# Banded attention heads of a hybrid transformer layer, put into one written order, with the division behind the values

## The chip, the cores and the metric

The kernel runs on one core of a Trainium2 chip. The metric is the device time of one launch in microseconds (us), the median of the runs. Engines are named as in the profile: PE (TensorE matmul), PEld (its weight load), DVE (VectorE), ACT (ScalarE), POOL (GpSimd) and SP (SyncE, which here only issues transfers).

## The reference, cut to what matters

One layer over 512 latent tokens with 256 context tokens: a modulated norm and one input projection, differential attention (group A, 4 heads), banded attention (group B, 8 heads of 64 columns, 2 key heads), one output projection, a second norm, a router that takes 4 of 32 experts, the experts, a last norm. The change lies in group B:

```python
def window_gqa_latent(q, k, v, k_ctx, v_ctx, sink):      # blocks of 128 queries
    ...
    s_loc = jnp.einsum('bnqkgd,bnjkd->bnkgqj', qbk, kband)       # own block and its neighbours
    s_ctx = jnp.einsum('bnqkgd,bjkd->bnkgqj', qbk, k_ctx)        # 256 context tokens
    ...
    s_loc = jnp.where(valid[None, :, None, None], s_loc, MASK_VALUE)
    ...
    p = jax.nn.softmax(jnp.concatenate([s_loc, s_ctx, sink_col], axis=-1), axis=-1)
    p_loc = p[..., :3 * W].astype(v.dtype)
    p_ctx = p[..., 3 * W:-1].astype(v.dtype)
    o = (jnp.einsum('bnkgqj,bnjkd->bnqkgd', p_loc, vband)
         + jnp.einsum('bnkgqj,bjkd->bnqkgd', p_ctx, v_ctx))
    return o.reshape(B, S, WA_OUT)
```

`x = x + g1 * (concatenate([ya, yb]) @ w_out)` follows, and the router and the experts work on its norm.

## The kernel before

Group B is done in 16 units (n, m): n is the block of 128 queries (0 to 3), m the pair of heads (0 to 3). A unit has 512 keys (`nk`) at n = 0 and 3, and 640 at n = 1 and 2, in 4 or 5 blocks of 128 (256 context tokens and the band). Every 32-bit operand stands as a high part and a low part, so a product is made of several matmuls.

- `scores_B(n, m)`: for each of the two heads a score product of queries `qB` with the keys `kB`. The first matmul of a pair has 128 rows (high query and low query parts against the high keys), the second has 64 rows and takes the low keys, `kB[rw, 2]`. Masks (`mprev`, `mnext`) are added by matmuls with `identb`. The sink goes into column `nk` of the scores by a one-column copy, on DVE for one head and on ACT for the other. DVE takes the negated maximum (`nmB`), ACT the exponential with its sum (`pB`, `rsB`), DVE the reciprocal of the sum. Then `pB` is multiplied by it, one head on ACT and the other on DVE.
- `turn_B`: PE transposes `pB` in groups of two key blocks (8 transposes of 128x128 into one `tp` tile), ACT writes the high part `pTh`, DVE the low part `pTl`. There are two `tp` tiles.
- `mix_B`: PE multiplies the values `vB` with both parts into `o`.
- `put_B` after every second unit: ACT copies (`yB`), DVE adds, and both split the result into `two`, the left operand of the output projection.
- `out_proj(n, kb)` multiplies `two` by row block kb of `w_out`: 6 matmuls of 512 columns. The row blocks are loaded by SP into `wo` (two buffers), split by ACT (`CAST`) and DVE in `prep_out` into `wp` or `w`.
- Beside the units the loop carries the group-A output (`start_Y`), the second norm (`norm2`), the router (`route_T`, `route` with `choose`, `rank`) and the gates' bias (`turn_gates`, `start_acc`) of earlier query blocks.

The order on PE, DVE and ACT is set by a planner wherever `pinned[0]` is empty, and by the order of the code where it names engines (P, V, S). Before, it is empty in the loop over the units, and the planner also brings the scores of units (0,1) and (0,2), six of the eight `wo` splits and the first three `out_proj` into the last part of group A. After the loop come the rest of the router, the gathering of tokens, and the experts.

Of the kernel before, what the change touches and what calls it, by code (L numbers as in the profile page):

```python
# [10 lines left out]
F32 = mybir.dt.float32  # L11
F32R = mybir.dt.float32r
# [10 lines left out]
T = 512  # L23
# [14 lines left out]
def tile_block(ctx: ExitStack, tc: tile.TileContext, a: dict, out: bass.AP, dbg=None):  # L38
# [64 lines left out]
    def ps_pj():  # L103
        return ps.tile([128, 512], F32, name="pj", bufs=2)
# [704 lines left out]
    def scores_B(n, m):  # L809

        b0, b1 = max(n - 1, 0), min(n + 2, 4)
        L = (b1 - b0) * 128
        nk = C + L
        g = m // 2
        rw = slice(g * 64, g * 64 + 64)
        q = qT[n]
        own = n + m < KN["own"]
        if own:
            assert nk == 512
            sv = [ps_pj() for _ in range(2)]  # L820
        else:
            s = sc_tile(KN["sB"])
            sv = [s[:, 0:TA], s[:, TA:2 * TA]]
        for i in range(2):
            hd, s = 2 * m + i, sv[i]
            cuts = [(0, C), (C, nk)] if i == 1 or nk == 512 else [(0, C), (C, 512), (512, nk)]
            masks = []
            if n > 0:
                masks.append((mprev, C))
            if n < 3:  # L830
                masks.append((mnext, nk - 128))
            ksl = lambda x0, x1: slice(T + x0, T + x1) if x0 < C else slice(b0 * 128 + x0 - C, b0 * 128 + x1 - C)
# [6 lines left out]
            if not own and KN["snk"] == "P":  # L839
                PE.matmul(s[:, nk:nk + 1], ones3, sink3[:, hd:hd + 1], start=True, stop=True)  # L840
        nm = bp.tile([128, 2], F32, name="nmB", bufs=4)
        rs = bp.tile([128, 2], F32, name="rsB", bufs=4)
        w = nk if own else nk + 1
        for i in range(0 if own or KN["snk"] == "P" else 2):
            (V.tensor_copy if KN["snk"][i] == "V" else S.copy)(sv[i][:, nk:w], sinkB[:, 2 * m + i:2 * m + i + 1])
        for i in range(2):
            V.tensor_reduce(nm[:, i:i + 1], sv[i][:, 0:w], axis=AX.X, op=OP.max, negate=True)
        if own:
            es = bp.tile([128, 3, 2], F32, name="esB", bufs=1)
            V.tensor_scalar_mul(es[:, 0], sinkB[:, 2 * m:2 * m + 2], -1.0)  # L850
            V.tensor_tensor(nm, nm, es[:, 0], op=OP.min)
            V.tensor_add(es[:, 1], nm, sinkB[:, 2 * m:2 * m + 2])
            S.activation(es[:, 2], es[:, 1], AF.Exp)
        pp = []
        for i in range(2):
            p = bp.tile([128, 641], F32, name="pB", bufs=5)
            S.activation(p[:, 0:w], sv[i][:, 0:w], AF.Exp, bias=nm[:, i:i + 1], accum_out=rs[:, i:i + 1])
            pp.append(p)
        if own:
            V.tensor_add(rs, rs, es[:, 2])  # L860
        V.reciprocal(rs, rs)
        for i in range(2):
            if KN["scB"][i] == "S":
                S.activation(pp[i][:, 0:nk], pp[i][:, 0:nk], AF.Copy, scale=rs[:, i:i + 1])
            else:
                (V if KN["scB"][i] == "V" else G).tensor_scalar(pp[i][:, 0:nk], pp[i][:, 0:nk], rs[:, i:i + 1], 1.0,
                                                             op0=OP.mult, op1=OP.mult)
        return pp, [4, 5] + list(range(b0, b1))

    def turn_B(pp, bl):  # L870

        w = len(bl) * 256
        tp = ps_tp().rearrange("p a b -> p (a b)")
        for i, x in enumerate(bl):
            for j in range(2):
                PE.transpose(tp[:, (2 * i + j) * 128:(2 * i + j + 1) * 128], pp[j][:, x * 128:(x + 1) * 128], ident)
        pt = pair(bp, [128, 512], "pT", 2)
        split(pt[0][:, 0:w], pt[1][:, 0:w], tp[:, 0:w])
        return pt
# [8 lines left out]
    def put_B(g, o, y):  # L888
# [40 lines left out]
    cur = scores_B(0, 0)  # L929
# [72 lines left out]
    Gt = lp.tile([128, E], F32, name="Gt")  # L1002
# [10 lines left out]
    fill = lp.tile([128, E * 3], F32, name="fill")  # L1013
    V.memset(fill, 0.0)
# [42 lines left out]
    def norm2(t):  # L1057
        t1 = lp.tile([128, D], F32, name="t1", bufs=2)
        for f in range(2):
            add_out(t, f, t1)  # L1060
        late = V if t == 3 else G
        gp2(t1, x1[t], G2B, OP.mult)
        sq = lp.tile([128, 4, 128], F32, name="ya", bufs=1).bitcast(BF16).rearrange("p a b -> p (a b)")
        ss = lp.tile([128, 1], F32, name="ss2", bufs=2)
        rs = lp.tile([128, 1], F32, name="rs2", bufs=2)
        S.activation(sq, x1[t], AF.Square, accum_out=ss)
        rstd_of(rs, ss, D)

        rt[t] = t1, rs, late
# [53 lines left out]
    def enter_slots(t):  # L1123
        eq, mi, ge, gs, pr = rt.pop(t)
        pk = lp.tile([128, 4, E], F32, name="pk")
# [13 lines left out]
        V.tensor_mul(eq, eq, val[:, :, 1:2].to_broadcast([128, 4, E]))  # L1139
        V.tensor_reduce(Gt, eq.rearrange("p k e -> p e k"), axis=AX.X, op=OP.add)  # L1140
# [29 lines left out]

    for i, (n, m) in enumerate(units):
        nxt = scores_B(*units[i + 1]) if i < 15 else None
        if m % 2 == 0:
            o = ps_o()
        pp, blocks = cur
        if m == 0 and n > 0:
            start_Y(n)
        if n == 0 and m == KN["ys"][0]:
            start_Y(n, slice(0, KN["yh"]))
        if n == 0 and m == KN["ys"][1]:  # L1180
            start_Y(n, slice(KN["yh"], 4))
# [4 lines left out]
        pts = [turn_B(pp, bl) for bl in bls[:2]]
        for k, bl in enumerate(bls):
            if k == 2:
                pts.append(turn_B(pp, bl))
            if k < len(fill):  # L1190
                out_proj(fill[k][0], [fill[k][1]])
            mix_B(m, pts[k], bl, blocks, o)
        cur = nxt
        if m % 2 == 1:
            put_B(m // 2, o, Yt[n][1])
# [3 lines left out]
        if n == 0 and m == 2:  # L1199
            router_vectors()  # L1200
# [4 lines left out]
        if n > 0:  # L1205
            (norm2, route_T, route, rank)[m](n - 1)
# [651 lines left out]
```

## Time and profile before

| | us |
|---|---|
| median of 3 runs (lowest, highest) | 1682.74 (1678.67, 1683.17) |
| the profiled execution, its own time | 1678.89 |
| its span | 1677.1 |
| start of the scores of unit (0,1) | 285.87 |
| last output of group A is stored (`YA_d<-y`) | 309.61 |
| last low part of the banded heads (`two<-yB`) ends | 456.54 |
| first matmul of the experts | 485.85 |

Times in rows are microseconds from the start of the span. A row of the timeline gives start, length, engine, line, operation, tiles and shapes, and in brackets how long the engine had stood idle and what released it. Almost every row has line 52, the helper that records the operations, so one goes by the names of tiles. Matmuls are pipelined: the length of a single one holds its way through the array; what it costs in a stream is the length of a row with many of them by their count.

### The profile page before, as it was taken

How to read it: one execution, taken by the hardware profiler on the slowest of the kernel's cores; microseconds unless marked ns; L12 is line 12 of the kernel's file. 1: busy time of each engine (PE TensorE's matmuls, PEld its weight loads, DVE VectorE, ACT ScalarE, POOL GpSimd, SP SyncE). 2: the span in 40 equal slices, each digit the busy share in tenths (PEclk: the TensorE clock that was granted, in tenths of full speed). 3: DMA queues.
4: the chain of work that ended last, by engine and by line, in shares of the span. 5: the costliest groups of instructions: out<-in, count | busy, mean ns of one | idle time of the engine just before them, and what ended most of it. 6: DMA issues, size and time to landing. Idle time of an engine off the chain costs nothing. (4 is left out here: it accounts for less than half of the span.)

```text
span 1677.1 us, 20947 instructions
## 1 busy us (share of the span) xinstructions
PE 1601.9 (96%) x7464; PEld 1283.1 (77%) x7464; DVE 1482.5 (88%) x1753; ACT 1093.5 (65%) x1406; POOL 213.6 (13%) x136
## 2 busy tenths in 40 slices
PE   7899997899889999999999999999999999999995
PEld 2686775677677888888888888888888888888884
DVE  6888887556778999999999999999999999999995
ACT  6544434445556767777776777776777777677763
POOL 0000001012330111111111111111111111111011
PEclk9899997879979999999999999999999999999998
DMA  9534325611579999999999999999999999999974
GB/s 350 173 92 132 108 88 149 184 45 47 193 244 380 353 367 369 357 377 372 374 362 366 360 369 380 383 362 366 369 362 369 374 374 361 367 355 370 357 295 128
DMA packets 115698, 494.11 MB, mean 295 GB/s; under 512 B 16385, under 2 KB 39082, under 8 KB 68418
## 3 DMA queue, kind: packets, MB, share of 16 engines
q1 hardware_dynamic: 99090, 456.44, 71.2%
q0 software_dynamic: 14192, 29.00, 8.4%
q10 hardware_dynamic: 2304, 7.24, 1.2%
q8 instruction: 61, 1.00, 0.2%
q14 instruction: 51, 0.42, 0.1%
HBM read 472.91 MB, written 27.57 MB: 298 GB/s over the span
## 5 line engine op out<-in xcount | busy, mean ns | idle before, releaser
L52 PE MATMUL h<-two 128*128 128x512 f32 x1694 | 421.5, 400 | 3.0 <-ACT two L52 3.0
L52 PEld LDWEIGHTS h<-two 128*128 128x128 f32 x1694 | 315.3, 189 | 74.3 <-ACT two L52 3.9
L52 PE MATMUL h<-wp,two 128*128 128x512 f32 x1338 | 334.7, 400 | 4.1 <-DVE pk L52 4.1
L52 DVE TENSOR_TENSOR two<-wp,two 128x1024 fp32r<-128x1024 f32 x254 | 300.8, 1219 | 7.5 <-ACT two L52 7.4
L52 PEld LDWEIGHTS h<-wp,two 128*128 128x128 f32 x1338 | 249.1, 190 | 58.2 <-ACT two L52 4.3
L52 ACT CAST two<-wp 128x1024 fp32r<-128x1024 f32 x254 | 258.0, 1049 | 17.0 <-PE y L52 14.6
L52 DVE TENSOR_TENSOR wp<-wp 128x1024 fp32r<-128x1024 f32 x176 | 205.5, 1219 | 2.9 <-ACT wp L52 2.9
L52 DVE TENSOR_TENSOR two<-w,two 128x1024 fp32r<-128x1024 f32 x170 | 200.2, 1219 | 2.3 <-ACT two L52 2.3
L52 POOL DMA_INDIRECT acc<-ys,slot_i x31 | 105.5, 3403 | 704.6 <-DVE ys L52 704.6
L52 ACT CAST wp<-wp 128x1024 fp32r<-128x1024 f32 x176 | 176.2, 1050 | 12.2 <-PE y L52 7.1
L52 ACT CAST two<-w 128x1024 fp32r<-128x1024 f32 x170 | 170.2, 1049 | 13.3 <-PE y L52 10.5
L52 PE MATMUL y<-two,ah 128*128 128x512 f32 x556 | 174.6, 395 | 0.8 <-DVE w L52 0.8
L52 PE MATMUL y<-wp,ah 128*128 128x512 f32 x468 | 147.1, 395 | 0.4 <-DVE wp L52 0.4
L52 DVE TENSOR_TENSOR wp<-w,wp 128x1024 fp32r<-128x1024 f32 x104 | 125.5, 1218 | 8.4 <-ACT wp L52 8.3
L52 PEld LDWEIGHTS y<-two,ah 128*128 128x128 f32 x556 | 104.4, 188 | 26.1 <-DVE w L52 1.2
L52 ACT CAST wp<-w 128x1024 fp32r<-128x1024 f32 x104 | 108.7, 1049 | 23.4 <-PE pj L52 10.3
L52 ACT CAST ah<-tpm 128x512 fp32r<-128x512 f32 x64 | 37.6, 588 | 123.1 <-PE tpm L52 123.1
L52 PE MATMUL y<-two,al 128*128 128x512 f32 x278 | 109.9, 395 | 0.0
L52 PEld LDWEIGHTS y<-wp,ah 128*128 128x128 f32 x468 | 88.2, 188 | 21.3 <-DVE wp L52 0.6
L52 DVE TENSOR_TENSOR wp<-wchunk,wp 128x1024 fp32r<-128x1024 f32 x82 | 98.2, 1218 | 0.0
L52 PE MATMUL pj<-xh,wp 128*128 128x512 f32 (+1 forms) x320 | 91.7, 364 | 1.9 <-ACT xf L52 1.0
L52 PE MATMUL y<-wp,al 128*128 128x512 f32 x234 | 92.4, 395 | 0.0
(333 smaller groups left out, 2350.1 us busy)
## 6 DMA issues: line engine op xcount, KB each, us to landing
wp<-in_w_gate_up_dram SPq DMA_DIRECT2D x140, 1024.0 KB
w<-in_w_gate_up_dram SPq DMA_DIRECT2D x85, 1024.0 KB
wp<-in_w_down_dram SPq DMA_DIRECT2D x75, 1024.0 KB
w<-in_w_down_dram SPq DMA_DIRECT2D x43, 1024.0 KB
wchunk<-in_w_gate_up_dram SPq DMA_DIRECT2D x31, 1024.0 KB
wm<-in_w_mod_dram SPq DMA_DIRECT2D x64, 256.0 KB
wchunk<-in_w_down_dram SPq DMA_DIRECT2D x10, 1024.0 KB
w<-in_w_in_dram SPq DMA_DIRECT2D x14, 512.0 KB
```

The costliest lines, as they stand in the source:

```text
L52: i = f(*args, **kwargs)
```

## The change

- The scores become a class: `head` (matmuls of one head), `max`, `exp`. The low keys are copied once into `klB`, 128 rows with zeros in the half of the other key head, so both matmuls of a pair have 128 rows and the full query operand. The copies are two on ACT and two memsets on POOL, ahead of the loop.
- The sink goes into column `nk` by a matmul of one column (`sink3`, `ones3`); the two copies are gone. Only unit (0,0) still treats the sink apart.
- `pB` is not multiplied any more. `put_B` takes the reciprocal of four sums at once, PE makes four transposes of the spread reciprocals, and DVE multiplies `yB` by them (two of 64x256). `pB` has 4 buffers in place of 5.
- In the loop PE, DVE and ACT follow the order of the code (`pinned[0] = "PVS"`): the scores of the next unit first, then the transposes of this one, then output projection and values. `norm2` is cut in two, `rank` comes after `put_B`, `router_vectors` moves to unit (0,3).
- Some small tiles share memory (`fill`, `zt` and `pk` with `hT`, `Gt` with `lg`).

The diff, cut:

```diff
-                PE.matmul(s[:, x0:x1], q[rw, hd], kB[rw, 2, ksl(x0, x1)], start=False, stop=not mk)
+                PE.matmul(s[:, x0:x1], q[:, hd], klB[:, g, ksl(x0, x1)], start=False, stop=not mk)
...
-            (V.tensor_copy if KN["snk"][i] == "V" else S.copy)(sv[i][:, nk:w], sinkB[:, 2 * m + i:2 * m + i + 1])
...
-            if KN["scB"][i] == "S":
-                S.activation(pp[i][:, 0:nk], pp[i][:, 0:nk], AF.Copy, scale=rs[:, i:i + 1])
-            else:
-                (V if KN["scB"][i] == "V" else G).tensor_scalar(pp[i][:, 0:nk], pp[i][:, 0:nk], rs[:, i:i + 1], 1.0,
-                                                             op0=OP.mult, op1=OP.mult)
...
+        rs = sums[n, g]
+        V.reciprocal(rs, rs)
+        rb = ps_tp()
+        for j in range(4):
+            PE.transpose(rb[:, j, :], rs[:, j:j + 1].to_broadcast([128, 128]), ident)
...
+        V.tensor_mul(yb[0:64], yb[0:64], rb[0:64, 0::2])
+        V.tensor_mul(yb[64:128], yb[64:128], rb[64:128, 1::2])
...
+    pinned[0] = "PVS"
     for i, (n, m) in enumerate(units):
...
+        if nxt:
+            for k in range(2):
+                nxt.head(k)
+            for k in range(2):
+                nxt.max(k)
+        ts = [Turned(pp, bl) for bl in bls[:2]]
+        for k in range(2):
+            ts[k].high()
+            if nxt:
+                nxt.exp(k)
+        for k in range(2):
+            ts[k].low()
+        if m != 1:
+            for f in fill[0:1]:
+                out_proj(f[0], [f[1]])
+        mix_B(m, ts[0].pt, bls[0], blocks, o)
...
+        for k in range(1, len(bls)):
+            mix_B(m, ts[k].pt, bls[k], blocks, o)
...
+        if m % 2 == 1:
+            put_B(n, m // 2, o, Yt[n][1])
+        if n > 0 and m == 3:
+            rank(n - 1)
```

What stands on ACT in units (0,0) and (0,1), where the output weights of row blocks 2 to 5 are split. In the change, from the split of group A's output on (`wp` and `w` are the split weights, `wo` the loaded ones):

```order
L935 CAST two<-ya 128x384 [waits DMAHW7_49,DMAHW2_49,DMAHW0_49]
L52 CAST wp<-wo 128x1024 [waits DMAHW5_49]
L52 CAST wp<-wo 128x1024 [waits DMAHW6_49]
L52 CAST pTh<-tp 128x512 [waits DVE_49,PE_49]
L52 ACTIVATE pB,rsB<-sc,nmB 128x513 [waits DVE_49]
L52 CAST pTh<-tp 128x512 [waits PE_49,Activation_49]
L52 ACTIVATE pB,rsB<-sc,nmB 128x513
L52 CAST wp<-wo 128x1024 [waits DMAHW3_49]
L52 CAST w_2827<-wo 128x1024 [waits DMAHW4_49]
L52 COPY yB<-o 64x256 [waits PE_49]
```

Before, these splits stand among the last work of group A (`aTh` is group A's):

```order
L52 CAST wp<-wo 128x1024 [waits DMAHW6_49]
L52 CAST wp<-wo 128x1024 [waits DMAHW7_49]
L52 ACTIVATE pB<-pB,rsB 128x512 [waits DVE_49,Activation_49]
L52 CAST aTh<-tp 128x512 [waits PE_49]
L52 CAST aTh<-tp 128x512 [waits PE_49,Activation_49]
L52 COPY sc<-sinkB 128x1 [waits DVE_49,Activation_49]
L52 CAST w_2860<-wo 128x1024 [waits DMAHW1_49]
```

Six splits have moved from group A into the first three units of the loop, each with its wait for a transfer ahead of the banded heads' own work.

The loads themselves on SP, in the change, from the last fills of the router's memory on (`slot_d` and `acc` are filled from `hT`):

```order
L988 DMA shc<-mod_d 128x4x2 [waits DMAHW2_49]
L994 DMA t_2681<-in_b_down_dram 32x1024 [waits DMAHW3_49]
L994 DMA t_2681<-in_b_down_dram 32x1024 [waits DMAHW4_49]
L994 DMA t_2681<-in_b_down_dram 32x1024 [waits DMAHW5_49]
L1039 DMA slot_d<-hT 128x4x96 [waits DMAHW6_49,DVE_49]
L1039 DMA slot_d<-hT 128x4x96 [waits DMAHW7_49]
L1039 DMA slot_d<-hT 128x4x96 [waits DMAHW0_49]
L1039 DMA slot_d<-hT 128x4x96 [waits DMAHW1_49]
L1057 DMA acc<-hT 256x1x512 [waits DMAHW2_49]
L919 DMA wo<-in_w_out_dram 128x1024 [waits DMAHW3_49,DVE_49]
L919 DMA wo<-in_w_out_dram 128x1024 [waits DMAHW4_49,DVE_49]
```

And before, around the last store of group A:

```order
L904 DMA wo<-in_w_out_dram 128x1024 [waits DMAHW7_49,DMAHW5_49,DVE_49]
L450 DMA mod_d<-mr 1x512 [waits DMAHW0_49,DVE_49]
L904 DMA wo<-in_w_out_dram 128x1024 [waits DMAHW6_49,DVE_49]
L904 DMA wo<-in_w_out_dram 128x1024 [waits DMAHW7_49,DMAHW2_49,DVE_49]
L904 DMA wo<-in_w_out_dram 128x1024 [waits DMAHW1_49,DVE_49]
L723 DMA YA_d<-y_2589 128x512 [waits DMAHW4_49,DVE_49]
L916 DMA ya<-YA_d 128x128 [waits DMAHW4_49]
L949 DMA x_2660<-in_x_dram 128x1024 [waits PE_49,DMAHW0_49,Activation_49,Pool_49]
```

The loads of row blocks 4 to 7 stood ahead of that store, and the first two of them now stand behind it, behind all the fills.

The third place is DVE at the end of a query block, here unit (1,3) of the change, from the last lower halves to the next unit's maxima, with the middle cut by leaving out the rows of `rank` between the two pieces:

```order
L52 TENSOR_TENSOR pTl<-tp,pTh 128x256 [waits Activation_49]
L52 SCALAR_TENSOR_TENSOR lg<-tp,rs_3269,brB 128x32 [waits PE_49,Pool_49]
L52 MAX mx<-lg 128x8 [waits DVE_49]
L52 MAX_INDEX mi<-mx,lg 128x8 [waits DVE_49]
L52 TENSOR_TENSOR eq<-iotaE,mi 128x128 [waits DVE_49]
L52 TENSOR_REDUCE selb<-eq 128x32 [waits DVE_49]
L52 TENSOR_SCALAR ng<-mx 128x1
L52 SCALAR_TENSOR_TENSOR t_3166<-t_3166,rs_3269,sh2B 128x1024
L52 RECIPROCAL rsB<-rsB 128x4
L52 TENSOR_TENSOR yB<-o,yB 64x256 [waits PE_49,Activation_49]
```

```order
L52 TENSOR_REDUCE lg<-eq 128x32 [waits DVE_49]
L52 CAST g_2694<-lg 128x32 [waits DVE_49]
L52 CAST g_2694<-lg 128x32
L52 TENSOR_TENSOR g_2694<-lg,g_2694 128x32 [waits DVE_49]
L52 TENSOR_REDUCE nmB<-sc 128x1 [waits PE_49]
L52 TENSOR_REDUCE nmB<-sc 128x1
L52 TENSOR_TENSOR pTl<-tp,pTh 128x512 [waits Activation_49] x2
```

Before, the planner puts the choice, the lower halves and the maxima between one another (`lg`, `mx`, `eq` are the choice, `selb` and `pos` the router's):

```order
L52 SCALAR_TENSOR_TENSOR lg<-tp,rs_3538,brB 128x32 [waits PE_49]
L52 MAX mx<-lg 128x8 [waits DVE_49]
L52 MAX_INDEX mi<-mx,lg 128x8 [waits DVE_49]
L52 TENSOR_SCALAR ng<-mx 128x1
L52 TENSOR_TENSOR eq<-iotaE,mi 128x128 [waits DVE_49]
L52 TENSOR_TENSOR pTl<-tp,pTh 128x512 [waits Activation_49]
L52 TENSOR_REDUCE selb<-eq 128x32 [waits DVE_49]
L52 RECIPROCAL gs<-gs 128x1 [waits Activation_49]
L52 COPY sc<-sinkB 128x1 [waits PE_49]
L52 TENSOR_SCALAR val<-ge,gs 128x4 [waits DVE_49]
L52 TENSOR_TENSOR pTl<-tp,pTh 128x512 [waits Activation_49]
L52 TENSOR_REDUCE nmB<-sc 128x1 [waits Activation_49]
```

In the change the next unit's maxima stand behind the whole choice, `put_B` and `rank`.

## Rows read from the trace of the kernel before

**Rows 1.** Busy time of each engine in stretches of the span: the stretch, its length, then busy time and (count) of PE, PEld, DVE, ACT and POOL, TensorE's granted clock as a share of full, the DMA share and GB/s. Three stretches of the banded loop, and the experts.

```profile
309.60:360.00 50.40, 46.24 (x208) 34.75 (x209) 29.92 (x64) 23.46 (x54) 2.95 (x8) 0.77 0.59 158
360.00:407.00 47.00, 46.20 (x250) 36.64 (x248) 29.78 (x72) 24.10 (x57) 13.21 (x10) 0.96 0.12 40
407.00:456.50 49.50, 44.44 (x254) 35.06 (x255) 34.92 (x94) 27.66 (x66) 14.12 (x11) 1.00 0.43 152
485.80:1650.00 1164.20, 1161.28 (x5220) 950.09 (x5221) 1106.91 (x1043) 845.94 (x922) 153.96 (x69) 1.00 0.97 361
```

**Rows 2.** Waits of PE and of SP's queue in the experts' stretch (485.8 or 486 to 1650): who waited for whom, us in total, times, longest.

```profile
PE h L52 <- DVE pk L52: 4.1, 1, 4.1
...
SPq L1257 <- DVE two L52: 325.2, 129, 6.7
```

**Rows 3.** PE in the loop, 376 to 395 us and 417 us, rows of the timeline: units (2,1), (2,2) and (3,1).

```profile
377.45 1.30 PE L52 MATMUL sc<-kB,qB 128*128 128x256 f32 x4
...
378.73 0.56 PE L52 MATMUL sc<-kB,qB 128*128 128x128 f32 x2
...
379.26 1.42 PE L52 MATMUL sc<-kB,qB 128*128 128x256 f32 x4
...
385.03 1.03 PE L52 MATMUL tp<-ident,pB 128*128 128x128 f32 x8
...
389.69 0.28 PE L52 MATMUL o<-pTl,vB 128*128 128x256 f32 x1
389.81 0.28 PE L52 MATMUL o<-pTh,vB 128*128 128x256 f32 x1
...
394.35 2.97 PE L52 MATMUL pj<-wp,two 128*128 128x512 f32 x12
...
415.45 0.97 PE L52 MATMUL tp<-wr,hT 128*128 128x32 f32 x8
```

**Rows 4.** PE at the end of group A, rows of the timeline; `pj<-kB,qB` are the scores of unit (0,0), `sc<-kB,qB` those of (0,1) and (0,2), `pj<-wp,two` is output projection, `tp<-ones,sqo` belongs to group A's last norm.

```profile
272.39 4.15 PE L52 MATMUL pj<-kB,qB 128*128 128x256 f32 x8 [1.52 <-DMA qB<-qB_d]
...
285.87 1.21 PE L52 MATMUL sc<-kB,qB 128*128 128x256 f32 x4
...
288.32 0.36 PE L52 MATMUL o<-aTl,va 128*128 128x256 f32 x1
...
296.68 1.32 PE L52 MATMUL sc<-kB,qB 128*128 128x256 f32 x4 [0.68 <-ACT pB L52]
...
299.72 1.91 PE L52 MATMUL pj<-wp,two 128*128 128x512 f32 x4
...
302.47 3.43 PE L52 MATMUL pj<-wp,two 128*128 128x512 f32 x14
305.73 0.95 PE L52 MATMUL tp<-ones,sqo 128*128 128x1 f32 x8
```

**Rows 5.** SP's queue from 290 us on, rows of the timeline (the last store of group A, the transfer that follows the fills, and the filling of `acc`), and ACT's last split before.

```profile
290.43 6.45 SPq L904 DMA_DIRECT2D wo<-in_w_out_dram  x3
309.61 0.33 SPq L723 DMA_DIRECT2D YA_d<-y  x1
...
327.50 2.06 SPq L916 DMA_DIRECT2D ya<-YA_d  x4
...
300.46 1.04 ACT L52 CAST w<-wo 128x1024 fp32r<-128x1024 f32 x1 [1.40 <-DMA wo<-in_w_out_dram]
```

**Rows 6.** Groups of DVE by form, 285.6 to 456.5 us: operation, tiles, shapes, count, busy us, mean ns of one, idle before.

```profile
L52 DVE TENSOR_TENSOR pTl<-tp,pTh 128x512 fp32r<-128x512 f32 x32 | 21.8, 686 | 10.5 <-ACT pTh L52 10.3
L52 DVE TENSOR_REDUCE nmB<-sc 128x1 f32<-128x641 f32 x16 | 12.4, 816 | 0.7 <-ACT sc L52 0.7
...
L52 DVE TENSOR_TENSOR yB<-o,yB 64x256 f32<-64x256 f32 x16 | 6.7, 422 | 7.9 <-ACT yB L52 7.5
L52 DVE TENSOR_SCALAR pB<-pB,rsB 128x640 f32<-128x640 f32 x8 | 5.8, 724 | 0.1
...
L52 DVE SCALAR_TENSOR_TENSOR t<-t,rs,sh2B 128x1024 f32<-128x1024 f32 x3 | 3.9, 1285 | 1.6 <-PE tp L52 1.6
...
L52 DVE TENSOR_TENSOR pTl<-tp,pTh 128x256 fp32r<-128x256 f32 x8 | 3.3, 414 | 0.5 <-ACT pTh L52 0.5
```

**Rows 7.** Groups of ACT by form in the same stretch, same columns.

```profile
L52 ACT CAST pTh<-tp 128x512 fp32r<-128x512 f32 x32 | 18.2, 585 | 27.1 <-PE tp L52 26.9
L52 ACT ACTIVATE pB<-sc,nmB 128x641 f32<-128x641 f32 x16 | 12.7, 797 | 4.9 <-DVE nmB L52 4.3 <-PE tp L52 0.5
...
L52 ACT ACTIVATE pB<-pB,rsB 128x640 f32<-128x640 f32 x8 | 6.7, 833 | 3.0 <-DVE rsB L52 3.0
...
L52 ACT CAST two<-t 128x1024 fp32r<-128x1024 f32 x3 | 3.4, 1131 | 0.0
```

**Rows 8.** DVE, rows of the timeline: first and last of the router's choice (5 of them and the one for `ng`) and of its ranking in the loop (`rank`, 10 with those that stand apart), and the loop's last row.

```profile
376.97 0.25 DVE L52 SCALAR_TENSOR_TENSOR lg<-tp,rs,brB 128x32 f32<-128x32 f32 x1 [1.35 <-PE tp L52]
...
378.44 0.37 DVE L52 TENSOR_REDUCE selb<-eq 128x32 bf16<-128x128 f32 x1
...
384.66 0.18 DVE L52 TENSOR_TENSOR pos<-tp,selb 128x32 f32<-128x32 f32 x1
...
386.28 0.17 DVE L52 TENSOR_TENSOR g<-Gt,g 128x32 fp32r<-128x32 f32 x1
...
456.11 0.43 DVE L52 TENSOR_TENSOR two<-yB,two 128x256 fp32r<-128x256 f32 x1
```

More of the change, by code (lines that the diff above doesn't have):

```diff
@@ L807, in tile_block @@
     V.tensor_sub(sink3[64:65], sinkr, sink3[32:33])
[L809 to L820, printed above, removed]
-        else:
[L822 to L825, printed above, removed]
-            cuts = [(0, C), (C, nk)] if i == 1 or nk == 512 else [(0, C), (C, 512), (512, nk)]
[L827 to L832, printed above, removed]
+    klB = bp.tile([128, 2, TA], F32R, name="klB")
@@ new lines, in tile_block, with __init__, head @@
+    for g in range(2):
+        rw, ro = slice(g * 64, g * 64 + 64), slice(64 - g * 64, 128 - g * 64)
+        G.memset(klB[ro, g].bitcast(F32), 0.0)
+        S.copy(klB[rw, g], kB[rw, 2].bitcast(F32))
+    class Scores:
+        def __init__(self, n, m):
+            self.n, self.m = n, m
+            self.b0, b1 = max(n - 1, 0), min(n + 2, 4)
+            self.blocks = [4, 5] + list(range(self.b0, b1))
+            self.nk = len(self.blocks) * 128
+            self.own = n + m == 0
+            if self.own:
+                self.sv = [ps_pj() for _ in range(2)]
+            else:
+                s = sc_tile(KN["sB"])
+                self.sv = [s[:, 0:TA], s[:, TA:2 * TA]]
+            self.w = self.nk if self.own else self.nk + 1
+            self.nm = bp.tile([128, 2], F32, name="nmB", bufs=4)
+            if m % 2 == 0:
+                sums[n, m // 2] = bp.tile([128, 4], F32, name="rsB", bufs=3)
+            self.rs = sums[n, m // 2][:, m % 2 * 2:m % 2 * 2 + 2]
+            self.pp = []
+        def head(self, i):
+            n, m, nk, s = self.n, self.m, self.nk, self.sv[i]
+            hd, g, q = 2 * m + i, m // 2, qT[n]
+            cuts = [(0, C), (C, nk)] if i == 1 or nk == 512 else [(0, C), (C, 512), (512, nk)]
+            masks = ([(mprev, C)] if n > 0 else []) + ([(mnext, nk - 128)] if n < 3 else [])
+            ksl = lambda x0, x1: slice(T + x0, T + x1) if x0 < C else slice(self.b0 * 128 + x0 - C, self.b0 * 128 + x1 - C)
@@ L868, in scores_B, with max @@
[L868 to L879, printed above, removed]
+        def max(self, i):
+            V.tensor_reduce(self.nm[:, i:i + 1], self.sv[i][:, 0:self.w], axis=AX.X, op=OP.max, negate=True)
@@ new lines, in tile_block, with __init__, high, low @@
+    sums = {}
+    class Turned:
+        def __init__(self, pp, bl):
+            self.w = len(bl) * 256
+            self.tp = ps_tp().rearrange("p a b -> p (a b)")[:, 0:self.w]
+            for i, x in enumerate(bl):
+                for j in range(2):
+                    PE.transpose(self.tp[:, (2 * i + j) * 128:(2 * i + j + 1) * 128], pp[j][:, x * 128:(x + 1) * 128], ident)
+        def high(self):
+            self.pt = pair(bp, [128, 512], "pT", 2)
+            S.copy(self.pt[0][:, 0:self.w], self.tp)
+        def low(self):
+            V.tensor_tensor(self.pt[1][:, 0:self.w], self.tp, self.pt[0][:, 0:self.w].bitcast(F32), op=OP.subtract)
@@ L928, in tile_block @@
         pass
-    cur = scores_B(0, 0)
+    cur = Scores(0, 0)
+    for i in range(2):
+        cur.head(i)
+    for i in range(2):
+        cur.max(i)
+    cur.sinks()
+    for i in range(2):
+        cur.exp(i)
+    V.tensor_add(cur.rs, cur.rs, cur.es[:, 2])
     for f in later:
@@ L1169, in store_acc @@
         nc.gpsimd.dma_start(acc[t * 128:(t + 1) * 128, :], x1[t])
+    pinned[0] = "PVS"
     for i, (n, m) in enumerate(units):
-        nxt = scores_B(*units[i + 1]) if i < 15 else None
+        nxt = Scores(*units[i + 1]) if i < 15 else None
         if m % 2 == 0:
             o = ps_o()
[L1175 to L1181, printed above, removed]
+        pp, blocks = cur.pp, cur.blocks
         fill = [(n - 1, 6), (n - 1, 7)] if m == 0 else [(n, 2 * m - 2), (n, 2 * m - 1)]
-        if n == 0:
-            fill = [(0, kb) for kb in KN["f0"][m]]
+        if n + m == 0:
+            fill = []
         bls = [list(range(x, min(x + 2, len(blocks)))) for x in range(0, len(blocks), 2)]
[L1186 to L1195, printed above, removed]
+        if nxt:
[14 more added lines that the diff above has]
+        mix_B(m, ts[0].pt, bls[0], blocks, o)
+        if len(bls) > 2:
+            ts.append(Turned(pp, bls[2]))
+            ts[2].high()
+            ts[2].low()
+        if m == 0:
+            start_Y(n, slice(0, 4 if n else 3))
+        if (n, m) == (0, 2):
+            start_Y(n, slice(3, 4))
         if n == 0 and m < 3:
```

75 lines of the change are left out of this document (39 added, 36 removed).

## The prediction

> **What bounds the kernel now.** I read the busy time by stretches first [rows 1]. In the experts PE is busy 1161 of 1164 us; it waits 4.1 us once, and the loads there wait for buffers that DVE frees [rows 2]. So nothing in that stretch takes up a shift: what the banded loop gains or loses is carried to the end one for one. The question is when the loop ends, now at 456.11 + 0.43 = 456.5 us [rows 8]. From 360 to 456.5 us PE is busy 90.6 of 96.5 us at a clock of 0.96 to 1.00, and before that 46.2 of 50.4 at 0.77 [rows 1]: PE is the loop's bound, in the planner's order. That speaks for a change that takes work from PE. But the change also replaces the order, and an order by hand on three engines that wait for each other can cost more than the work. So I sum the work, and then walk the new order row by row.
>
> **PE's work.** Durations at full clock, by the row's pitch [rows 3]: 0.12 per 256 columns (389.69 to 389.81), 0.25 per 512 columns (2.97 for 12; 0.233 without the run-out of the last one), 0.11 per transpose (1.03 for 8 less the run-out). The scores' pairs of 128 and 64 rows cost 1.30 for four matmuls of 256 columns, 0.32 each, where the pitch of 256 columns is 0.12. With 128 rows in both, a pair of heads at 512 keys costs 8 x 0.116 = 0.93 plus masks and sinks 0.4 = 1.3, in place of 2.6; at 640 keys 1.7 in place of 3.3 (377.45 to 380.73 by the three rows: 1.30 + 0.56 + 1.42). The saving is 1.3 to 1.6 a unit, some 23 us in 16 units. Bounds: nothing, if the step between row counts isn't what those rows show, and 25.
>
> By a page that speaks against this edit, the Trainium skill, "TensorEngine Tiling (Array Packing)", section "When to Use Tiling", a contraction of 64 rows or fewer should be tiled, for up to twice the speed; by it the old low-key matmuls cost half and the padded ones cost about 4 us more in all. The rows at 0.32 per matmul say the opposite here.
>
> The division costs PE 8 x 4 transposes of 0.11 = 3.5. Sum for the new loop: scores, transposes and values 3.1 (512 keys) or 4.0 (640) a unit, 12 matmuls of output projection 2.8 in 15 units, the divisors 3.5, router 16 x 0.12 + 0.9 in three blocks and 1.9 once, gates 1.2: **113 us**.
>
> **DVE and ACT.** Removed: 16 scalings of `pB` on each (0.72 and 0.83 at 640 keys [rows 6, 7]) and 15 sink copies each. Added on DVE: 16 multiplications of 64x256, taken at the 0.42 of the additions of that shape [rows 6]; 6.7 us in place of 9.6 and 2.4. Both engines stay below PE's sum, but they are in PE's path at every step. The building of `klB` (two copies, two memsets) lies ahead of the loop in group A; I cost it at nothing, covered by group A's waits, 0 to 2.
>
> **When the loop begins.** Before, the end of group A carries the scores of (0,1) and (0,2) (285.87 to 288.32, and as long again from 296.68) and 18 matmuls of output projection (1.91 + 3.43, behind which `tp<-ones,sqo` stands) [rows 4]: 10.2 us of PE. The scores of (0,0), 4.15, move behind group A's last scores. Together at most 14.3; at least 8, since part of it filled waits. I take 13: the last store of group A comes at 309.6 - 13 = 296.6 [rows 5], and the loop's first scores, which stand just ahead of it, at **296**.
>
> **The walk of one unit.** At 640 keys, from the next unit's scores: PE scores 1.7, transposes of this unit 0.9, to 2.6; DVE maxima 2 x 0.78, to 3.4; ACT upper half 0.5, exponential 0.8 (from 3.5), upper half 0.5, to 4.9; DVE lower half 0.66, to 5.6; third upper half behind the second exponential, to 6.0; its lower half 0.4, to 6.4; values, 6.7 [rows 6, 7]. PE's own work in that time is 6.8. An undisturbed unit is thus even. But whatever else stands on DVE or ACT ahead of the maxima goes straight into the next unit.
>
> **Where it is disturbed.** At the end of a query block DVE has the choice (1.4, rows of 0.25 to 0.37), the norm's 1.29, the reciprocal, two additions that wait for ACT's copies (which stand behind 1.13 of `two<-t`), two multiplications, a lower half, then the ranking (1.8 and some that stood apart, 2.2), all ahead of the next maxima [rows 6, 7, 8]: about 10 us between lower halves and maxima, while PE has 4 to 5 us to do. Walked from the start of unit (1,3): the router's matmuls end at 7.6, the choice 9.2, the norm 10.6, `two<-t` on ACT 11.8 and its two copies 12.6, additions and multiplications 14.0, the lower half 14.9, position and ranking 17.6, the maxima of the unit after next 19.1, the first lower half of (2,0) 19.8. PE began the scores of (2,1) at 11.4, as an even unit asks, was through with them, the transposes (one of which waits for a `tp` tile that DVE frees at 15.4) and the first projection at 17.3, and stands until 19.9. At m = 1 four rows of 0.69 and `put_B` stand there. Walked through all units in this way, PE waits 22 us at values (for lower halves), 7 at output projection, 7 at the divisors' transposes, 4 at the next unit's transposes, 5 in the router and 3 at the gates: 49 us. With 3.5 from PE's last matmul to the last lower half the loop is 113 + 49 + 3.5 = **165 us**.
>
> **The late loads.** ACT must split row blocks 4 and 5 in unit (0,1), ahead of `put_B` and of the next unit's upper half. Their loads now stand on SP behind the fills. Before, the transfer behind those fills was issued 17.9 us after group A's store (309.61 to 327.50), and a load was usable 3.4 us after its issue (the last of three at about 297, used at 300.46) [rows 5]. With 0.4 more for the fill of `acc`, 18.3, and 3.4 they can be split at 296.6 + 21.7, or a little later since the fills are still in flight: 23 after the loop's begin. The walk reaches them at 12 and everything waits: the end moves by 11 to 12; I take **12**, bounds 0 (if the fills go through faster) and 12.
>
> **The clock.** Idle PE loses clock: 0.77 in a stretch where it was 92% busy [rows 1], and here it is busy for 70%. With all of PE's durations a fifth longer the walk ends 9 later. I take 3, bounds 0 and 9.
>
> **Sum.** 296 + 165 + 12 + 3 = 476, against 456.5: 19.5 later. The profiled execution takes 1678.9, so 1698.4 by it; the median of the runs is 1682.7, 3.8 above that execution, so **1702** for the median.
>
> **The rivals.**
> - *The fixed order keeps PE full.* ACT waited 27 us for PE's transposes before [rows 7], so PE was what the others waited for, and 23 us of it are gone; an undisturbed unit is even. If half the walk's waits don't occur (24.5) and the loads cost 6, the end is 296 + 113 + 24.5 + 3.5 + 6 + 3 = 446: 10.5 earlier, 1672. If PE is as full as before (94%, 7 of waits) and the loads cost nothing, it's 296 + 113 + 7 + 3.5 = 419.5, 1646. It decides below about 30 us of waits. For it: the long lists of waits. Against it: DVE's stretch of 10 us has no other work in between. Chance 0.27.
> - *As the forecast, with the loads in time.* 296 + 165 + 3 = 464: 1690, still slower. With the slow clock and the loads late, 482: 1708. If group A ends only 8 earlier, 5 more: 1713. These stand within the forecast, chance with it 0.60.
> - *Gain and loss even out*: waits of about 30 us and the loads in time or half late; within 0.3% (5 us, about what a measurement of this kernel can tell from no change). Chance 0.10.
> - *The 64-row step isn't what costs*, so the padded keys save nothing: each unit's maxima come 1.3 to 1.6 later, up to 23 more, 1725. Rows 3 speak against it. Chance 0.03.
>
> The rule on 64 rows cited above from the Trainium skill would have the sign of this last case. The Trainium skill, "TensorEngine Tiling (Array Packing)", section "PSUM Bottleneck", also warns that faster matmuls leave the copy out of PSUM as the limit: before, the upper halves on ACT waited for PE [rows 7], so it was not yet so.
>
> **How the numbers follow.** Likeliest: 1702. Ends of the forecast: 1687 (loads in time, early begin) to 1713. The range must leave out no more than 0.2: from 1664, which takes in most of the first rival, to 1714. Faster 0.27, within 0.3% 0.10, slower 0.63.
>
> **What the profile will show.** Scores of `klB` at 0.12 a matmul with no step on PEld. The last store of group A at about 297. ACT waiting for a `wo` transfer for about 11 us near 308 to 320. `nmB` on DVE late behind `g<-lg` in units (2,0) and (3,0), and PE waiting for `pTl` there. PE's busy share in the loop down to about 70%. The loop's last `two<-yB` near 476. I am wrong if PE stays above 85% busy there, if the loop is below 155 us long, or if the first experts' matmul moves by another amount than the loop's end.

## The result and the profile after

The changed kernel takes 1698.34 us in the median of 4 runs (1696.25 to 1701.23), the kernel before beside it 1680.70 (4 runs): ratio 1.0104, with a 95% interval of 1.0081 to 1.0127. It is slower by about 17.5 us, inside the range and close to the forecast of 1702.

The busy time by stretches of the changed kernel, with the columns of [rows 1]: two stretches of its banded loop, the whole loop (293.80 to 474.60), and the experts.

```profile
295.00:321.00 26.00, 15.51 (x67) 12.26 (x65) 11.71 (x21) 10.15 (x19) 0.86 (x6) 0.70 0.91 287
...
360.00:407.00 47.00, 39.37 (x224) 31.88 (x223) 26.19 (x60) 17.43 (x40) 9.02 (x9) 0.86 0.17 51
...
293.80:474.60 180.80, 143.37 (x814) 117.88 (x812) 101.38 (x209) 72.96 (x160) 28.05 (x27) 0.87 0.36 113
...
502.00:1667.00 1165.00, 1159.36 (x5218) 947.24 (x5219) 1108.06 (x1050) 848.04 (x926) 154.61 (x69) 1.00 0.97 361
```

Where the planner had PE busy in 46.2 of 47 us [rows 1], the written order has 39.4 busy in the same 47 us. PE stands idle for 37 us in the loop. From the first matmul of the experts to the end of the span it takes 1190.4 us (1694.5 less 504.06), before 1191.3 (1677.1 less 485.85), so next to nothing was lost or won there.

The last row of the loop on DVE, which answers to the last of [rows 8]:

```profile
474.20 0.42 DVE L52 TENSOR_TENSOR two<-yB,two 128x256 fp32r<-128x256 f32 x1 [0.47 <-ACT two L52]
```

It ends at 474.62, 18.1 us later than before. The first matmul of the experts comes at 504.06, 18.2 later than 485.85. The shift is carried over whole.

Where the 18.1 us come from is read best from one place in group A, which both kernels reach within 0.3 us of each other (250 us), to the end of the loop: the kernel before, the changed kernel, and the changed arithmetic in the planner's order (the run u_planner below).

```profile
250.00:456.54 206.54, 184.37 (x904) 140.15 (x903) 136.13 (x304) 103.57 (x226) 36.34 (x36) 0.87 0.39 120
250.00:474.62 224.62, 175.23 (x963) 140.82 (x961) 131.00 (x267) 92.78 (x197) 35.40 (x36) 0.86 0.37 114
250.00:448.83 198.83, 166.17 (x959) 139.67 (x958) 130.62 (x276) 92.95 (x197) 36.29 (x37) 0.87 0.41 126
```

In the changed kernel PE is busy for 9.1 us less than before, and idle for 27.2 us more (49.4 against 22.2). In the planner's order the same arithmetic leaves it idle for 32.7.

SP's queue around the last store of group A and the late loads, answering to [rows 5]:

```profile
294.96 0.34 SPq L723 DMA_DIRECT2D YA_d<-y  x1
...
311.08 0.60 SPq L1057 DMA_DIRECT2D acc<-hT  x1
311.78 1.44 SPq L919 DMA_DIRECT2D wo<-in_w_out_dram  x2
```

ACT in units (0,0) and (0,1), without the rows that read the sums out:

```profile
301.52 2.00 ACT L52 CAST wp<-wo 128x1024 fp32r<-128x1024 f32 x2
...
307.35 0.70 ACT L52 ACTIVATE pB<-sc,nmB 128x513 f32<-128x513 f32 x1
...
316.75 1.04 ACT L52 CAST wp<-wo 128x1024 fp32r<-128x1024 f32 x1 [8.61 <-DMA wo<-in_w_out_dram]
318.09 1.04 ACT L52 CAST w<-wo 128x1024 fp32r<-128x1024 f32 x1 [0.29 <-DMA wo<-in_w_out_dram]
319.16 0.74 ACT L52 COPY yB<-o 64x256 f32<-64x256 f32 x2
```

Group A ends 14.7 us earlier: its end carries no work of the loop any more. The loads of row blocks 4 and 5 are issued 16.8 us behind the store, and ACT stands 8.6 us with the copies of `put_B` and the next upper halves behind it. DVE's low parts of the split stand behind ACT's, the reciprocal behind them, and PE waits for that:

```profile
320.62 1.09 PE L52 MATMUL tp<-ident,rsB 128*128 128x128 f32 x4 [7.42 <-DVE rsB L52]
```

DVE from unit (1,3) into (2,0), the place of the prediction's walk; unit (1,3) begins at 370.00 with the scores of the next:

```profile
377.77 0.25 DVE L52 SCALAR_TENSOR_TENSOR lg<-tp,rs,brB 128x32 f32<-128x32 f32 x1 [1.45 <-PE tp L52]
...
378.91 0.38 DVE L52 TENSOR_REDUCE selb<-eq 128x32 bf16<-128x128 f32 x1
...
379.26 1.27 DVE L52 SCALAR_TENSOR_TENSOR t<-t,rs,sh2B 128x1024 f32<-128x1024 f32 x1
...
382.50 0.88 DVE L52 TENSOR_TENSOR yB<-o,yB 64x256 f32<-64x256 f32 x2 [1.87 <-ACT yB L52]
383.41 0.87 DVE L52 TENSOR_TENSOR yB<-yB,tp 64x256 f32<-64x256 f32 x2
...
387.45 0.19 DVE L52 TENSOR_TENSOR g<-lg,g 128x32 fp32r<-128x32 f32 x1
387.56 1.55 DVE L52 TENSOR_REDUCE nmB<-sc 128x1 f32<-128x641 f32 x2
389.02 0.68 DVE L52 TENSOR_TENSOR pTl<-tp,pTh 128x512 fp32r<-128x512 f32 x1
```

And PE there:

```profile
370.00 0.28 PE L52 MATMUL sc<-kB,qB 128*128 128x256 f32 x1
...
381.61 0.36 PE L52 MATMUL sc<-kB,qB 128*128 128x256 f32 x1
381.81 0.28 PE L52 MATMUL sc<-klB,qB 128*128 128x256 f32 x1
...
384.42 0.63 PE L52 MATMUL tp<-ident,pB 128*128 128x128 f32 x4 [0.90 <-DVE yB L52]
...
387.54 0.28 PE L52 MATMUL o<-pTh,vB 128*128 128x256 f32 x1
389.76 0.39 PE L52 MATMUL o<-pTl,vB 128*128 128x256 f32 x1 [1.94 <-DVE pTl L52]
```

The scores of (2,1) stand ready at 383.5 us, and their maxima begin at 387.56, because DVE works through choice, `put_B` and ranking first. PE waits for the lower half behind those maxima.

### The profile page after: what moved, and what is told of

It is laid out like the page before. It is cut to its first block, busy times and chain, and to the rows that moved or that the text cites. A ratio compares the mean times of both kernels' runs of the same rounds, so it can differ in the third digit from the quotient of the medians.

```text
span 1694.5 us, 21053 instructions
## 1 busy us (share of the span) xinstructions
PE 1586.1 (94%) x7526; PEld 1277.4 (75%) x7526; DVE 1480.0 (87%) x1729; ACT 1082.9 (64%) x1377; POOL 215.5 (13%) x138
## 5 line engine op out<-in xcount | busy, mean ns | idle before, releaser
L52 ACT CAST two<-wp 128x1024 fp32r<-128x1024 f32 x254 | 258.0, 1049 | 17.0 <-PE y L52 14.3
```

The costliest lines, as they stand in the source:

```text
L52: i = f(*args, **kwargs)
```

## The experiments

The theory: the written order costs more in waits (work ahead of what PE needs, on DVE and ACT, and the late loads) than the score pairs give back. The rivals: the parts of the change cost by themselves, or the row counts are worth nothing. Each ratio is against the kernel before on the same chip; differences between two ratios are turned into us with 1681.

**The planner's order for the changed arithmetic (u_planner).**

```diff
-    pinned[0] = "PVS"
+    pinned[0] = ""
     for i, (n, m) in enumerate(units):
```

> The changed kernel with pinned[0] empty in the loop, so the planner orders PE, DVE and ACT there again; all parts of the arithmetic stay changed. Theory (the written order costs): the planner fills PE's gaps and takes scores and splits into group A's end; the loop ends at about 456.5 + 3.5 (divisors) - 20 (scores) = 440 or a little later, time 1660 to 1672, below the kernel before. Rival (the parts cost: the divisors' transposes hold tp tiles, exponentials and values hang closer together): above the kernel before, 1685 to 1700. Rival (the code's order binds the planner too, since scores stand ahead in the code): 1675 to 1690.

Measured: 1668.88 us, ratio 0.9919 (0.9889 to 0.9950): faster than the kernel before, and 31 us below the changed kernel. Its busy time in the loop, and DVE's last row of it:

```profile
350.00:400.00 50.00, 45.01 (x267) 38.43 (x268) 31.94 (x72) 23.43 (x55) 10.03 (x8) 0.90 0.17 48
```

```profile
448.41 0.42 DVE L52 TENSOR_TENSOR two<-yB,two 128x256 fp32r<-128x256 f32 x1
```

The time is in the band of the theory, though the loop ends at 448.8 and not at 440: PE is busy 90% of this stretch, not 98% as in the middle stretch of [rows 1]. The order alone, with what the planner moves ahead of the loop, turns a gain into a loss.

**Which engine's order (p_P, p_VS).** The order of the code holds for PE alone in one run, for DVE and ACT in the other.

```diff
-    pinned[0] = "PVS"
+    pinned[0] = "P"        # p_P
+    pinned[0] = "VS"       # p_VS
```

> The changed kernel with only PE in the order of the code inside the loop; the planner orders DVE and ACT. Theory A (the waits come from work that stands in line on DVE and ACT ahead of what PE needs): DVE and ACT get free, most of the 29 us between the changed kernel (1698) and the same arithmetic in the planner's order (1669) comes back: 1670 to 1680. Theory B (PE's own order is at fault: scores, then transposes, then a projection that can't step aside): 1688 to 1700.

> The changed kernel with DVE and ACT in the order of the code inside the loop and PE in the planner's. Theory A (DVE's and ACT's lines): stays at 1690 to 1700. Theory B (PE's order): comes down to 1670 to 1682. If both this and the run with PE alone come down, it is the three together, each waiting for the next.

Measured: PE alone 1676.98, ratio 0.9963 (0.9947 to 0.9978); DVE and ACT alone 1704.24, ratio 1.0123 (1.0099 to 1.0147). With DVE and ACT free, 24 of the 31 us come back; with PE free, none. The first is within theory A's band; the second lies above it by 4 (its interval overlaps that of the changed kernel). In the second run ACT waits still longer for the first late load:

```profile
321.90 1.04 ACT L52 CAST wp<-wo 128x1024 fp32r<-128x1024 f32 x1 [12.31 <-DMA wo<-in_w_out_dram]
```

So what costs is the written order on DVE and ACT. PE's own order costs the smaller part, if any (0.9963 against 0.9919, with intervals that touch). The 24 us hold the late loads too: in the first run the planner puts all eight splits ahead of the loop again, the last at 294.29, with group A's store at 303.84.

```profile
294.29 1.04 ACT L52 CAST w<-wo 128x1024 fp32r<-128x1024 f32 x1 [2.02 <-DMA wo<-in_w_out_dram]
```

**The late loads (w_pool, w_early).** First another queue for the loads, then earlier splits:

```diff
-        dma(w, wo[:, kb, :])
+        (dma if kb < 4 else nc.gpsimd.dma_start)(w, wo[:, kb, :])
```

```diff
-    for kb in range(KN["np"], 2):
+    for kb in range(KN["np"], 4):
...
-        if n == 0 and m < 3:
+        if n == 0 and m in (1, 2):
```

> The changed kernel with the loads of the output weights' row blocks 4 to 7 issued by POOL, not by SP, so they no longer stand behind the fills; nothing else. Theory (the loads are late because they stand in line on SP): the first is issued when its buffer is free, near 306, and ACT's wait in (0,1) falls from 8.6 us to under 2, none in (0,2); time 1688 to 1692. Rival (the DMA engines are full with the fills, busy share 0.91 from 295 to 321 us, so any load there is slow): the wait falls to 4 to 7 us, time 1693 to 1697.

> The changed kernel, with the output weights' row blocks 2 and 3 split ahead of the loop, so that the loads of 4 and 5 stand ahead of the last store of group A on SP. Theory (late loads and waits of the fixed order outweigh what PE saves): ACT's wait for wo in unit (0,1), 8.6 us in the changed kernel, goes, DVE's and PE's waits behind it too; group A ends 1 to 3 us later for the two splits; the time falls from 1698 by 6 to 10, to 1688 to 1692, still above the kernel before. Rival (the loads only fill a time in which the pipeline would wait anyway, for instance for transfers of the router's tables): within 3 us of 1698. Rival (parts of the change cost, not the order): within 3 us of 1698.

Measured: w_pool 1692.03, ratio 1.0053 (1.0032 to 1.0074), 8.6 us below the changed kernel; w_early 1695.62, ratio 1.0078 (1.0050 to 1.0105), 4 us, whose interval overlaps that of the changed kernel. ACT in w_pool, and POOL's issues there:

```profile
312.57 1.05 ACT L52 CAST wp<-wo 128x1024 fp32r<-128x1024 f32 x1 [2.86 <-DMA wo<-in_w_out_dram]
314.95 1.04 ACT L52 CAST w<-wo 128x1024 fp32r<-128x1024 f32 x1 [1.34 <-DMA wo<-in_w_out_dram]
```

```profile
305.71 0.62 POOL L919 DMA_DIRECT2D wo<-in_w_out_dram  x1 [6.08 <-DVE wp L52]
...
296.00:320.00 24.00, 16.66 (x75) 13.79 (x74) 12.90 (x25) 10.55 (x20) 3.08 (x10) 0.71 0.91 274
```

The last row is the stretch around these loads, with the DMA share at 0.91. Issued when its buffer is free, the load can be used 6.2 us after the issue's end (306.33 to 312.57); in [rows 5] it took 3.6 (296.88 to 300.46), at a DMA share of 0.45. Both readings hold in part: the time lies with the first, the wait (4.2 us are left) with the second, so standing in line on SP was not all of it. That the rest comes from busy DMA engines fits the share, but is only argued: the issuing engine changed too, and no run loads from POOL without the fills. In w_early the load came in time, but group A's store came 3.0 us later, at 297.94. The two splits are not all of that: where nothing ahead of the store was changed (r_late below) it comes at 296.50, so 1.5 us can lie between two profiles. The next pair of loads was late in turn:

```profile
325.51 1.05 ACT L52 CAST w<-wo 128x1024 fp32r<-128x1024 f32 x1 [5.43 <-DMA wo<-in_w_out_dram]
```

The wait had moved by one unit. The expected 6 to 10 us did not come; the later store and the moved wait fit that, by their sizes.

**The low keys on 64 rows in the written order (k_64rows).**

```diff
-                PE.matmul(s[:, x0:x1], q[:, hd], klB[:, g, ksl(x0, x1)], start=False, stop=not mk)
+                PE.matmul(s[:, x0:x1], q[g * 64:g * 64 + 64, hd], kB[g * 64:g * 64 + 64, 2, ksl(x0, x1)], start=False, stop=not mk)
```

> The changed kernel with the low keys on 64 rows as before (kB and half of the query rows in place of klB), all else as changed. Theory (scores stand at the head of the chain of every unit): each unit's maxima come 1.3 to 1.6 us later, the loop grows by 15 to 23 us, 1713 to 1721. Rival (PE stands idle for 50 us in the loop, so what PE saves there is worth nothing): within 4 us of 1698. Rival by the rule that 64 rows are to be tiled: the scores get shorter and the time falls by up to 4.

Measured: 1716.59, ratio 1.0202 (1.0172 to 1.0232), 16.5 us above the changed kernel: the theory's band, and no sign of the rivals. The loop is 195.8 us long with PE busy for 168.9 of it, 25.5 more than in the changed kernel:

```profile
299.40:495.20 195.80, 168.90 (x814) 127.57 (x812) 101.81 (x210) 73.06 (x160) 28.04 (x27) 0.84 0.34 104
```

Of 25 us on PE 15 reach the loop's length; the other 10 fill time in which PE stood idle (26.9 us of it are left, of 37.4). That they reach it because the scores stand at the head of every unit is argued. The loop also begins 5.6 us later in this profile; unit (0,0)'s pairs, which stand ahead of it, take about 2 of that, the rest is open.

**The low keys on 128 rows alone, and the control (b_klB, b_mem).** The kernel before, with `klB` built and used as in the change; `pB` has 4 buffers and the small tiles share memory, to make room. The control has the same memory and builds `klB`, but multiplies with 64 rows.

```diff
-                PE.matmul(s[:, x0:x1], q[rw, hd], kB[rw, 2, ksl(x0, x1)], start=False, stop=not mk)
+                PE.matmul(s[:, x0:x1], q[:, hd], klB[:, g, ksl(x0, x1)], start=False, stop=not mk)
```

> The kernel before with one part of the change alone: the low keys on 128 rows (klB), with pB in 4 buffers and the small tiles sharing memory to make room, as in the change. Planner's order, division and sinks as before. Theory (PE is the bound of the loop in the planner's order, the score pairs cost 1.3 to 1.6 us a unit too much): loop 15 to 20 us shorter, time 0.9890 to 0.9920 of the kernel before (1664 to 1670 on the same chip). Rival (the planner's loop is bound by the evacuation of scores and transposes, and the gain of the same arithmetic in the planner's order came from the division): within 0.3% of the kernel before.

> The control for the low keys on 128 rows: the kernel before with klB built, pB in 4 buffers and the small tiles sharing memory, but the low keys' matmuls on 64 rows as before. If the row count is what gained (0.982): 0.997 to 1.004. If the planner's other order, which any edit brings, or the memory gained: 0.980 to 0.992.

Measured: b_klB 1652.89, ratio 0.9821 (0.9797 to 0.9846); control 1677.63, ratio 0.9987 (0.9964 to 1.0010), no difference. The row count is worth 28 us, more than the theory's band had (0.9890 to 0.9920); the control lies in its own. The planner makes its order anew for each kernel, and this pair can't part that from the row count; with the order written out (k_64rows) the row count is worth 16.5. b_klB is the fastest kernel of the study. PE in unit (2,1) of b_klB, which answers to the score rows of [rows 3]:

```profile
371.11 0.28 PE L52 MATMUL sc<-kB,qB 128*128 128x256 f32 x1
371.24 0.28 PE L52 MATMUL sc<-klB,qB 128*128 128x256 f32 x1
371.35 0.28 PE L52 MATMUL sc<-kB,qB 128*128 128x256 f32 x1
371.47 0.28 PE L52 MATMUL sc<-klB,qB 128*128 128x256 f32 x1
```

The pitch from start to start is 0.12; before, it was 0.31 (four such rows and a mask from 377.45 to 378.73). The loop ends at 430.9, 25.6 earlier than before and 22.9 earlier than in the control's profile, with PE busy for 26.5 us less than there (the control in the second row):

```profile
250.00:430.93 180.93, 154.75 (x908) 128.30 (x907) 136.45 (x305) 105.32 (x229) 37.24 (x38) 0.91 0.43 133
250.00:453.83 203.83, 181.29 (x901) 135.55 (x900) 134.24 (x303) 105.51 (x228) 37.81 (x38) 0.89 0.39 122
```

What in the 64-row form costs can be read a little further in group A of the kernel before. There the row counts change only after every second matmul; this row holds two of 64 rows, one of 512 and one of 256 columns, at full clock:

```profile
196.03 0.61 PE L52 MATMUL sc<-kl,q 64*128 64x512 f32 x2
```

The second starts 0.34 after the first, where 128-row matmuls of 512 columns follow at 0.23; where the first has 256 columns it is 0.22, not 0.12. So about half of the 0.19 that each matmul costs more comes with 64 rows though no count changes, and only what is left with the change.

**The other parts (b_div, b_sinkP, u_norm).** To b_klB the division behind the values was added, or the sinks by a matmul; and from u_planner the division was taken out (`pB` scaled again, the multiplications in `put_B` gone).

```diff
-'snk': 'VS'
+'snk': 'P'
```

```diff
-        V.reciprocal(rs, rs)
-        for i in range(2):
-            if KN["scB"][i] == "S":
...
+        V.tensor_mul(yb[0:64], yb[0:64], rb[0:64, 0::2])
+        V.tensor_mul(yb[64:128], yb[64:128], rb[64:128, 1::2])
```

> The kernel before with the low keys on 128 rows (0.982 of the kernel before) and, added to that, the division behind the values; planner's order and the code's old structure, sinks by copies. Theory (division behind the values costs: four transposes and a tp tile per put_B on PE's path, while the scalings it removes lay on DVE and ACT beside PE): 0.986 to 0.992. Rival (it saves: 16 scalings of 0.5 to 0.8 us leave DVE and ACT, and exponential to transpose gets shorter): 0.972 to 0.980.

> The kernel before with the low keys on 128 rows and, added to that, the sinks by a matmul of one column in place of the copies on DVE and ACT; division as before, planner's order. Theory (two copies of 0.16 stand between scores and maxima and ACT's waits for DVE's copy; a matmul of one column costs PE 0.04 to 0.07): 0.978 to 0.982. Rival (PE is the bound, so 30 matmuls cost it 2 us and more for weights): 0.983 to 0.985.

> The changed arithmetic and structure in the planner's order (0.992 of the kernel before), with the division undone: pB is scaled by ACT and DVE as before, behind the next unit's exponentials in the code. If the division is what costs the changed arithmetic against the low keys alone (0.992 against 0.982): 0.982 to 0.986. If it is the structure (scores of both heads in one piece, moved steps of the router, sinks): 0.990 to 1.000.

Measured: b_div 1662.66, ratio 0.9893 (0.9860 to 0.9926), 12 us above b_klB and in the theory's band; b_sinkP 1658.62, ratio 0.9871 (0.9835 to 0.9906), 8 above, with intervals that just overlap, and in neither expected band; u_norm 1660.34, ratio 0.9876 (0.9843 to 0.9909), 7 below u_planner, with intervals that overlap, and between the two expected bands. Neither part gained anything here. b_div has DVE and ACT busy for 3.7 and 10.8 us less than b_klB, whose row stands above beside the control's, up to the end of its own loop, and yet it is slower:

```profile
250.00:439.17 189.17, 157.59 (x937) 130.09 (x935) 132.80 (x295) 94.56 (x213) 37.54 (x38) 0.93 0.43 137
```

Its loop ends 8.2 us later, with PE busy for 2.8 and idle for 5.4 us more. The scalings lay beside PE's work, as the prediction had them, and their removal was no gain. That the four transposes and the `tp` tile of each `put_B` are what costs is only argued: each edit also gives the planner another order, and no run here separates the two.

**The ranking moved behind the next lower halves (r_late).**

```diff
-        if n > 0 and m == 3:
-            rank(n - 1)
...
+        if n > 1 and m == 0:
+            rank(n - 2)
```

> The changed kernel with the ranking of the router moved from the end of unit (n,3) behind the lower halves of the next unit (for block 2 behind the loop). Theory (DVE's work ahead of the maxima goes straight into the next unit): the maxima of the units behind (1,3), (2,3) come 2.4 us earlier, less what the ranking then holds up before turn_gates; time falls by 2 to 5, 1693 to 1696. Rival (PE or the transposes' tiles bind there): within 1.5 us of 1698, or up to 3 more because the gates come later.

Measured: 1701.96, ratio 1.0120 (1.0089 to 1.0152), not to be told from the changed kernel. The expected gain of 2 to 5 did not come. DVE, then PE, in unit (2,0) of this run:

```profile
387.64 1.56 DVE L52 TENSOR_REDUCE nmB<-sc 128x1 f32<-128x641 f32 x2
...
394.23 0.19 DVE L52 TENSOR_TENSOR g<-lg,g 128x32 fp32r<-128x32 f32 x1
```

```profile
394.56 0.42 PE L52 MATMUL tp<-ident,g 128*96 128x128 f32 x1 [3.01 <-DVE g L52]
```

The maxima now follow `put_B` at once, but the gates need the ranking, and in PE's written order they stand ahead of the projection and the rest of the unit: PE waits 3.0 us there. So "whatever stands ahead of the maxima goes into the next unit" was too narrow: here the ranking held PE up in the new place as well, since PE may not step past the gates.

## Why the prediction was right

- *The mechanism.* It had the written order cost more in waits than the score pairs give back. Shown: 27.2 us more of idle PE against 9.1 less of work up to the loop's end, and a gain of 0.9919 when only the order is the planner's.
- *One for one to the end.* Shown: 18.1 at the loop's end, 18.2 at the first experts' matmul, 17.4 at the span's end.
- *When the loop begins.* Forecast: store of group A at 296.6, first scores at 296. Measured: 294.96 and 293.8, which is 14.7 earlier where the prediction had at most 14.3; profiles differ by 1.5 there.
- *The walk of one unit.* Forecast for unit (1,3), counted from 370.0: choice 379.2, norm 380.6, additions and multiplications 384.0, ranking 387.6, maxima 389.1, first lower half 389.8, values 389.9. The rows above: choice 379.3, norm 380.5, multiplications 384.3, ranking 387.6, maxima 389.1, lower half 389.7, values 389.8. In this written order one unit could be walked with durations from the kernel before to a few tenths of a us.
- *The loop's length, right in part by luck.* Forecast 180 (165 + 12 + 3), measured 180.8. But the forecast had 113 us of work on PE and about 65 of idle PE (49 walked, 12 for the loads, 3.5 at the end), with 3 for the clock, and measured are 143.4 of work and 37.4 of idle time. Of the walked waits (the six items add up to 48, not 49) those at the next unit's transposes came out, 4 and 4.0; at values it was 11.0 in place of 22, nearly all for lower halves (the row below: us in total, times, longest); at output projection 1.2 in place of 7; in the router 2.9 in place of 5, at the gates 2.5 in place of 3. At the divisors it was 12.3 in place of 7, of which 7.4 are the late load's, so that the load's own term, 12, was too large as well: ACT waited 8.6, and w_pool took away 8.6 by the ratios, but 4 of the loop's length in its profile (store to end, 175.4 against 179.7).

```profile
PE o L52 <- DVE pTl L52: 10.0, 13, 1.9
```

- *The clock.* It was taken at 3. The loop ran at a granted clock of 0.87 in the mean and 0.70 in the stretch from 295 to 321 us. An estimate from that: between the two levels, 1 and 0.5 (2.4 and 1.2 GHz), 0.87 means about 47 us at the lower one, and with PE busy for 79% of them its work is some 19 us longer. That is most of the 30 us by which PE is busier than forecast; the rest is open. By the forecast's own walk, a fifth more work on PE moves the end by only 9, since the rest fills waits; that is one reason why the two errors, of 30 and 27 us, cancel. The rows don't bear out its step from busy share to clock: [rows 1] have 0.77 at 92% busy and 1.00 at 90%, and k_64rows has 0.84 at 86% where the changed kernel has 0.87 at 79%.
- *PE's busy share.* Forecast about 70%, measured 79% (143.4 of 180.8). It stays below the 85% from which I had called the forecast wrong.
- *The score pairs.* Forecast 1.3 to 1.6 a unit, some 23 in all. Measured 28 in the planner's order (b_klB against its control), 16.5 in the written one.
- *The rivals.* The written order didn't keep PE full: 37 us of idle PE in the loop. The point of 30 that I had named doesn't decide, though: without the load's 7.4 and the end's 3.7 the waits are 26, below it, and the kernel was slower all the same, since PE's work took 30 us more than the sum that the point came from. The rival that 64 rows aren't what costs fell with k_64rows and b_klB. The Trainium skill, "TensorEngine Tiling (Array Packing)", section "When to Use Tiling", would have short contractions tiled; here the 64-row form costs 28 us over the zero-padded one. No run sets two tiles to work side by side. The Trainium skill, same page, section "Key Properties", says that a change of tiling mode drains TensorE. The trace agrees only in part: 0.31 us against 0.12 per matmul fits it, but about half of the difference stands in group A's pairs of 64 rows too, where no count changes.
- *What it hadn't seen.* The forecast gave the division a price on PE alone, 3.5 us, and took the relief of DVE and ACT as harmless at worst. In the planner's order it went with 12 us more; of the 8.2 that its profile shows of them, 2.8 are work on PE, near the price, and 5.4 are waits. So the change held one part worth 28 us, other parts worth nothing or less, and an order that cost 31 (each between two runs; they need not add up).

## What to carry to other kernels

Ahead of a written order, list for each engine what stands between two units, and walk one unit with measured durations; here, where DVE and ACT carry the work of other stages too, a planner that may slip small rows between long ones was 31 us better. A sum that comes out is not yet a sum whose terms are right: compare busy and idle time apart. Try the parts of a large change one by one, each with a control for the memory that it brings: here one part, the low keys on 128 rows, was worth more than the whole. A transfer that is moved past a store may end up behind everything that waited for that store; look at the queue and not only at the engine.

## What the runs showed of the hardware

Matmuls of 256 columns whose row counts alternate between 128 and 64 follow each other at about 0.31 us, those with 128 rows throughout at 0.12, both at a granted clock of 0.99 or more, with half of the rows zero in every second one; I had expected the step, not that 28 us hang on it. Two 64-row matmuls behind each other (group A of the kernel before) stand 0.22 apart at 256 columns and 0.34 at 512, so the change of the row count is not all of the cost. A load of 512 KB was usable 3.6 us after its issue's end at a DMA share of 0.45 (issued by SP, the kernel before), and 6.2 us after it beside the fills at 0.91 (issued by POOL, w_pool).
